# A hybrid decoder step on eight cores: sample tile amid the prompt groups, paced loads, FFN buffers laid over mixer buffers, two planner settings

## The chip, the cores and the metric

The kernel runs on the 8 cores of one Trainium2 chip. Each core works on one sequence of the prompt and on its share of the sample tokens. The time is the device time of the slowest core. The fast runs of one kernel agree within 0.3% (the kernel before) to 0.8% (e_pw) here; some runs fall in a slower state, in which the cores of one die, sometimes of both, show a lower granted clock (the clock that TensorE was allowed). The engine with the most work is TensorE (the matmul engine); the others are VectorE (DVE), ScalarE (ACT), GpSimd (POOL) and SyncE (SP), which issues loads and stores, as GpSimd does.

## The reference, cut to what matters

```python
def _layer(h, pe, state, ...):                  # one layer, DEPTH = 1
    a = rmsnorm(h, norm_mix)
    z = a @ w_in                                # 1024 -> 3080: [u | v_g | q | k | v_m | o | i | f]
    u = gelu(u); vg = layernorm(gelu(vg), ...)  # vg of the last chunk is an output: o_Vp, o_Vs
    y_gm = _gmlp_mix(u, vg, ...)                # causal 128x128 mixing, 4 heads
    hm, state = _mlstm(q, k, vm, ig, lf, state, ml_len)   # matrix memory C (4 heads, 128x128)
    h = h + concat([y_gm, sigmoid(o) * rmsnorm(hm)]) @ w_out
    h = h + square(relu(rmsnorm(h, norm_ffn) @ w_up)) @ w_down      # 1024 -> 4096 -> 1024
    gate = sigmoid(rmsnorm(h, norm_ple) @ w_ple_gate)
    h = h + gate * (pe @ w_ple_proj)
    return h, state, vg
# then a final rmsnorm. Prompt: 8 x 2048 tokens, zero state. Sample: 128 x 8 tokens, carried state.
```

A core has 16 prompt tiles of 128 tokens and one sample tile of 16 sequences with 8 tokens each. The sample tile needs its carried memory `state_C` (`sC` below), which is 16 x 4 matrices of 128x128 in fp32.

## The kernel before

The 17 tiles go in two halves: 8 prompt tiles and the sample tile, then 8 prompt tiles. In a half, the mixer stages (input norm N, projections P, gates G, mixing M) run in groups of two tiles, then the FFN runs in four quarters of its width, and stage C (gate, final norm, output `y`) follows the last quarter.

The kernel is a program that plans a program. Every operation is put on a list; a greedy planner with a cost model then fixes one static order for each engine, and semaphores are placed after it. The planner has a model of loads and a number of accumulation banks (those that TensorE writes its results to) that each class of operations may hold; any edit of the kernel gives another order everywhere.

```python
            if o.dma:                                   # in Plan.schedule: one queue for all loads
                free[e] = s + o.cost
                d0 = max(free[e] + 1.0, dma_free)
                dma_free = d0 + o.nbytes / 170e3        # 170 GB/s on the bytes of the destination
                o.fin = dma_free + 1.2
...
        order = P.schedule(dict(P=3, M=4, N=1, U=3, D=2, C=2, X=2))    # banks by class; N: norm transposes
...
        SO = Arena(W_OFF + 32 * KB, W_OFF + 48 * KB)    # state buffers ON two weight slots (k, m)
        CSB = [SO.bf(16 * 130, ...) for _ in range(2)]
        R = Arena(0, W_OFF)                             # FFN and stage C, laid over A
        ...
        A3 = [R.bf(DM) for _ in range(2)]               # norm buffers of stage C
        A2T = R.bf(8 * 9 * 128, k8(8))                  # FFN input, nine tiles in one piece
        ABF = [R.bf(DM) for _ in range(2)]              # norm buffers of the FFN
        A = Arena(0, W_OFF)                             # mixer
        ...
        VO = A.f32(512)                                 # output vg, its own buffer
        ABA = [A.bf(DM) for _ in range(2)]              # norm buffers of the mixer
...
            groups = [sg[0:2], sg[2:4], sg[4:6], sg[6:8]] + ([sg[8:9]] if len(sg) > 8 else [])
            for gi_, grp in enumerate(groups):
                ...                                     # load_x, stage_N, stage_P, stage_G, stage_M
            load_q(0)                                   # FFN weights of quarter 0
```

Of the kernel before, what the change touches and what calls it, by code (L numbers as in the profile page):

```python
# [19 lines left out]
def _dsize(dt):  # L20
    return mybir.dt.size(dt)
# [102 lines left out]
class Emit:  # L124
# [112 lines left out]
    def op(self, eng, calls, reads, writes):  # L237
        deps, rr, wr = self._deps_for(reads, writes, eng)
        self._emit_waits(eng, self._waits(eng, deps))
# [14 lines left out]
        self._record(rr, wr, tok, eng)  # L254

    def dma(self, eng, kw, out, in_):
        deps, rr, wr = self._deps_for([in_], [out], "dma")
        i = self.dma_i[eng]
# [15 lines left out]
        self._record(rr, wr, tok, "dma")  # L274

# [33 lines left out]
class Op:  # L309
    __slots__ = ("eng", "dma", "calls", "reads", "writes", "cost", "nbytes", "idx", "rank", "preds", "succs", "npred",  # L310
                 "pts", "tset", "fin", "tready")
# [9 lines left out]
class Plan:  # L321
# [3 lines left out]
    def __init__(self):  # L325
        self.ops = []
        self.bufs = {}
        self.boost = 0

    def add(self, eng, calls, reads, writes, cost, dma=False, nbytes=0, tset=None):  # L330
# [4 lines left out]
        o.rank = o.idx - self.boost  # L335
# [6 lines left out]
    def _link(self, o):  # L342
        P = o.preds
        psr = {}
# [41 lines left out]
    def schedule(self, caps):  # L386
# [28 lines left out]
        while len(order) < n:  # L415
# [48 lines left out]
            if o.dma:  # L464
                free[e] = s + o.cost
                d0 = max(free[e] + 1.0, dma_free)
                dma_free = d0 + o.nbytes / 170e3
# [27 lines left out]
DM = 1024  # L495
# [9 lines left out]
def build():  # L505
# [29 lines left out]
    with ExitStack() as st:  # L535
# [78 lines left out]
        def dma(out, in_, eng="sp", **kw):  # L614
            nb = _nelem(out) * list(out.ap)[0][1] * _dsize(out.dtype)
            return P.add(eng, (out, in_, kw), [in_], [out], 0.9 if eng == "pool" else 0.06, dma=True, nbytes=nb)
# [83 lines left out]

        W_OFF = ARENA - 65536
# [12 lines left out]
        SO = Arena(W_OFF + 32 * KB, W_OFF + 48 * KB)  # L714
        CSB = [SO.bf(16 * 130, ("p (j e) -> p j e", dict(j=16)))[:, :, 0:129] for _ in range(2)]
        QTD = SO.bf(16 * 128, ("p (j t) -> p j t", dict(j=16)))

        R = Arena(0, W_OFF)
        WG = R.bf(8 * DM, k8(8))
        WP = R.bf(2 * DM, k8(2))  # L720
        NF = R.f32(DM)
        A3 = [R.bf(DM) for _ in range(2)]
        A3T = [R.bf(8 * 128, k8(8)) for _ in range(2)]
        PBF = [R.bf(PLE) for _ in range(2)]
        PTT = [R.bf(2 * 128, k8(2)) for _ in range(2)]
        TC = [R.f32(DM) for _ in range(2)]
        Z2 = R.off
        A2T = R.bf(8 * 9 * 128, k8(8))
        ABF = [R.bf(DM) for _ in range(2)]
        GT = [R.bf(8 * 384, k8(8)) for _ in range(2)]  # L730
        RL = [R.f32(384) for _ in range(2)]
        SU = Arena(Z2 - 18 * KB + 2 * KB, Z2)
        CSF = [SU.f32(8 * 129, ("p (j e) -> p j e", dict(j=8))) for _ in range(3)]
        KMK = SU.bf(8 * 128, ("p (j d) -> p j d", dict(j=8)))
        NOUT = SU.f32(64, ("p (h j) -> p h j", dict(h=4)))

        A = Arena(0, W_OFF)
# [9 lines left out]
        VO = A.f32(512)  # L747
        BROW = A.f32(512)
        SBS = A.f32(512, h4)
        KTOK = [A.bf(512, h4) for _ in range(3)]  # L750
        VAUG = [A.bf(4 * 130, h4)[:, :, 0:129] for _ in range(4)]
        UT = [A.bf(4 * 256, h4) for _ in range(2)]
        SGT = [A.bf(4 * 256, h4) for _ in range(2)]
        QT = [A.bf(4 * 256, h4) for _ in range(2)]
        KT = [A.bf(4 * 256, h4) for _ in range(2)]
        XH = [A.bf(512) for _ in range(3)]
        VN = [A.f32(512) for _ in range(2)]
        AT = [A.bf(8 * 256, ("p (k n) -> p k n", dict(k=8))) for _ in range(2)]
        ABA = [A.bf(DM) for _ in range(2)]


        dma(H[:, 0, :], xp[0:128, :])
        dma(GN[:], gains)
        dma(IDB[:], cident, eng="pool")

        def load_win(names):
            v = w_in.rearrange("(k p) n -> p k n", p=128)
# [519 lines left out]
```

## Time and profile before

| | before |
|---|---|
| median of 4 runs (range) | 1049.41 us (1047.43 to 1106.67, the last one slow) |
| profiled span, slowest core | 1052.3 us |
| TensorE busy | 895.6 us (85%) |
| TensorE idle | 157 us |
| first `y_p` store issued | 510.6 us |
| first FFN matmul (384 columns) | 279.69 us |

The prediction below shows the stretches in which TensorE stands idle. Two more lines of the page complete them. The first pair is the chain of waits that sets the end, by engine and by what it waited for; the third line, of the list of loads (the four that the mixer waits for), gives a load's kilobytes and its median time from issue to landing.

```profile
PE 75%; DMA 11%; DVE 6%; issue 4%; POOL 2%; ACT 1%; another core or an unknown queue 0%; DVEq 0%; POOLq 0%; ACTq 0%
PE pb L251 75%; DMA WGT<-wgate 5%; DMA AR<-sC 4%; DVE AR L251 3%; DMA AR<-psm 2%; ACT AR L251 1%; POOL SMALL L251 1%; DVE ROWX L251 1%; POOL AR L251 1%; DVE H L251 1%; DVE SMALL L251 0%; POOL AR L273 0%; DVE CST L251 0%; DVE ROWN L251 0%
...
AR<-sC POOLq DMA_DIRECT2D x4, 512.0 KB, 26.1
```

A quarter of this chain is not matmul work, and 11% of the span is waiting for loads: the gate weights at the start, the state `sC`, and the sample's `psm` (its per-layer embedding) at the handover between the halves.

One mark is used in all that follows: the issue of the first `y_p`. It divides a run into a **first part** (start, first mixer, first FFN) and a **second part** (handover, second mixer, second FFN, end). In the kernel before, these parts are 510.6 and 1052.3 - 510.6 = 541.7 us. The *handover* is the stretch in which the first half's stage C meets the second half's norms and projections; the *second transition* is that from the second mixer to the second FFN.

### The profile page before, as it was taken

The page shows a single profiled execution, that of the slowest core. Times are in us where ns is not written, and L with a number is a line of the kernel's source. Part 1 is how long each engine was busy: PE and PEld are TensorE (multiplying, and loading weights), DVE is VectorE, ACT ScalarE, POOL GpSimd, SP SyncE. Part 2 cuts the span into 40 slices and gives each one's busy share as a digit, 9 for nine tenths or more (in the row PEclk, how much of TensorE's full clock was granted, in tenths as well). Part 3 has the DMA queues.
Part 4 walks back from the last instruction along what each step waited for, and adds up shares of the span by engine and source line. Part 5 has one row for each costly group of instructions (what it writes and reads, how often), then busy time and mean ns, then how long its engine had stood idle before and what let it go on. Part 6 is the DMA issues. An engine that isn't in the chain of part 4 may idle for free.

```text
span 1052.3 us, 17095 instructions; the slowest of 8 cores (1034.6 to 1052.3 us)
## 1 busy us (share of the span) xinstructions
PE 895.6 (85%) x5875; PEld 535.8 (51%) x5875; DVE 587.3 (56%) x1092; ACT 383.5 (36%) x706; POOL 265.7 (25%) x383
## 2 busy tenths in 40 slices
PE   0588899622799999999998797799699999999994
PEld 0365577411554555555554476466355555555552
DVE  2184987912655744444666334899664444444665
ACT  2564544410521112213456444345451211213543
POOL 4141543712401201001133221556520101000221
PEclk9999999865899999999999699699799999999998
DMA  9993000989995917246239500005997725400121
GB/s 170 215 154 54 1 2 2 115 81 126 187 193 89 185 43 122 40 57 106 87 87 202 135 21 1 1 1 91 125 126 124 105 55 83 78 1 3 46 69 60
DMA packets 80769, 90.62 MB, mean 86 GB/s; under 512 B 13736, under 2 KB 62124, under 8 KB 80684
## 3 DMA queue, kind: packets, MB, share of 16 engines
q0 software_dynamic: 54304, 59.22, 40.3%
q1 hardware_dynamic: 26380, 30.32, 10.1%
q8 instruction: 48, 0.79, 0.3%
q14 instruction: 37, 0.30, 0.1%
HBM read 134.81 MB, written 13.93 MB: 141 GB/s over the span
## 4 chain that ended last, share of the span: by engine, by line
PE 75%; DMA 11%; DVE 6%; issue 4%; POOL 2%; ACT 1%; another core or an unknown queue 0%; DVEq 0%; POOLq 0%; ACTq 0%
PE pb L251 75%; DMA WGT<-wgate 5%; DMA AR<-sC 4%; DVE AR L251 3%; DMA AR<-psm 2%; ACT AR L251 1%; POOL SMALL L251 1%; DVE ROWX L251 1%; POOL AR L251 1%; DVE H L251 1%; DVE SMALL L251 0%; POOL AR L273 0%; DVE CST L251 0%; DVE ROWN L251 0%
## 5 line engine op out<-in xcount | busy, mean ns | idle before, releaser
L251 PE MATMUL pb<-AR 128*128 128x512 bf16 (+4 forms) x4924 | 837.9, 330 | 72.5 <-DMA AR<-sC 32.4
L251 PEld LDWEIGHTS pb<-AR 128*128 128x128 bf16 x4924 | 469.2, 99 | 408.4 <-issue 99.9
L251 ACT ACTIVATE AR<-pb 128x384 f32<-128x384 f32 (+5 forms) x349 | 176.4, 512 | 458.6 <-PE pb L251 377.3
L251 DVE TENSOR_TENSOR H<-H,pb 128x512 f32<-128x512 f32 x170 | 116.5, 685 | 143.1 <-PE pb L251 142.9
L251 DVE TENSOR_TENSOR AR<-AR 128x384 bf16<-128x384 f32 (+2 forms) x209 | 123.0, 591 | 113.9 <-ACT AR L251 113.3
L251 ACT ACTIVATE AR<-H 128x1024 bf16<-128x1024 f32 x68 | 71.5, 1052 | 65.8 <-DVE H L251 26.1
L251 PE MATMUL pb<-IDB,AR 128*128 128x128 bf16 x578 | 51.7, 234 | 51.2 <-ACT AR L251 34.8
L251 DVE TENSOR_TENSOR AR<-pb,GN 128x1024 bf16<-128x1024 bf16 x51 | 61.7, 1221 | 60.2 <-PE pb L251 59.8
L251 POOL TENSOR_SCALAR SMALL<-SMALL 128x1 f32<-128x1 f32 x85 | 22.8, 268 | 286.2 <-ACT AR L251 246.6
L251 POOL TENSOR_TENSOR SMALL<-SMALL,NEGH 128x1 f32<-128x1 f32 (+1 forms) x102 | 69.9, 686 | 37.2 <-DVE SMALL L251 18.3
L251 PEld LDWEIGHTS pb<-IDB,AR 128*128 128x128 bf16 x578 | 41.8, 105 | 65.8 <-issue 56.9
L251 ACT ACTIVATE AR<-H,SMALL 128x1024 bf16<-128x1024 f32 x51 | 58.1, 1145 | 32.3 <-POOL SMALL L251 32.0
L273 POOL DMA_DIRECT2D AR<-w_up x16 | 14.6, 914 | 148.6 <-PE pb L251 141.3
L251 DVE TENSOR_TENSOR AR<-pb,AR 128x258 f32<-128x258 f32 (+3 forms) x86 | 43.4, 521 | 2.9 <-PE pb L251 1.7
L251 ACT ACTIVATE AR<-pb,GSM 128x129 f32<-128x129 f32 x68 | 20.4, 369 | 51.0 <-PE pb L251 50.9
L251 DVE SCALAR_TENSOR_TENSOR AR<-AR,pb 128x512 f32<-128x512 f32 x34 | 23.2, 684 | 22.3 <-PE pb L251 11.5
L251 ACT ACT_TABLE_LOAD x24 | 30.8, 1283 | 11.5 <-PE pb L251 5.0
L251 ACT ACTIVATE AR<-AR 128x512 f32<-128x512 f32 x34 | 21.4, 629 | 31.9 <-DVE AR L251 31.4
L251 DVE SCALAR_TENSOR_TENSOR AR<-H,SMALL,AR 128x1024 f32<-128x1024 f32 x17 | 22.7, 1338 | 10.2 <-POOL SMALL L251 10.1
L251 POOL TENSOR_TENSOR AR<-AR,GROW 128x512 bf16<-128x512 f32 (+1 forms) x19 | 24.7, 1306 | 12.8 <-DVE AR L251 10.5
L273 POOL DMA_DIRECT2D AR<-w_in x12 | 10.8, 905 | 62.4 <-PE pb L251 62.3
L251 POOL TENSOR_TENSOR AR<-MSK,GSM 128x512 f32<-128x512 f32 x17 | 18.3, 1079 | 32.8 <-DVE GSM L251 32.8
(100 smaller groups left out, 437.0 us busy)
## 6 DMA issues: line engine op xcount, KB each, us to landing
AR<-w_up POOLq DMA_DIRECT2D x16, 1024.0 KB, 13.9
AR<-w_down POOLq DMA_DIRECT2D x16, 1024.0 KB, 15.6
AR<-w_in POOLq DMA_DIRECT2D x12, 1024.0 KB, 21.6
H<-xp SPq DMA_DIRECT2D x16, 512.0 KB, 10.5
y_p<-AR SPq DMA_DIRECT2D x16, 512.0 KB, 3.0
AR<-w_out POOLq DMA_DIRECT2D x2, 2048.0 KB, 50.8
AR<-sC SPq DMA_DIRECT2D x8, 512.0 KB, 16.9
o_Cs<-AR SPq DMA_DIRECT2D x8, 512.0 KB, 5.0
```

What stands on the lines that cost most here:

```text
L251: ins = getattr(e, name)(**kw)
L273: lambda e, out=out, in_=in_, sem=sem, kw=kw: e.dma_start(out=out, in_=in_, **kw).then_inc(sem, 16))
```

## The change

Its intent: load only what is wanted next and hold the rest until a mark is reached; move the sample tile before the last prompt group, with state buffers of its own, loaded ahead; lay the FFN's input over mixer buffers that come free early, so that the FFN can start while the mixer ends. It also changes the planner's model of loads and its number of norm banks. The diff, cut to its core:

```diff
-                dma_free = d0 + o.nbytes / 170e3
+                dma_free = d0 + o.nbytes / 290e3       # and nb = 4 bytes per element, the fp32 source
...
-        CSB = [SO.bf(16 * 130, ...) for _ in range(2)]      # on weight slots
-        A3, ABF, ABA: a pair of norm buffers for each of the three stages; VO, BROW: own buffers
+        AB = [LOW.bf(DM) for _ in range(2)]                 # ONE pair for all three
+        CSB = [A.bf(8 * 130, ...) for _ in range(2)]        # own, half a head each
+        B_ = Arena(P0, FO[1]);  A2T = [B_.bf(8 * 384, g3) for _ in range(2)]   # over AT and VN
+        B_ = Arena(FO[1], FO[0]);  GT = [...]; RL = [...]   # over u, o, q, k of the other parity
+        B_ = Arena(FO[0], XO);  A2T.append(B_.bf(8 * 384, g3)); ...
...
-                    dma(o_Vs if t["ty"] == 1 else o_Vp, VO)
+                    dma(o_Vs if t["ty"] == 1 else o_Vp, vn) # vn = VN, under the FFN's input
...
+                elif gi_ > 1:
+                    for t in grp:
+                        load_x(t, marks[gi_ - 2])           # wait for an earlier group's gelu
...
+                    load_win("v", after=nops[:1])           # nops: the scaling of a norm
+                    consts_a(nops[1:]);  wgate, load_win("o", after=nops[1:])
+                    load_win("qkm", after=nops);  w_out
+                if si == 0 and gi_ == 2:
+                    sample_prep(marks[1])                   # state tiles, their norms and constants
...
-            groups = [sg[0:2], sg[2:4], sg[4:6], sg[6:8]] + ([sg[8:9]] if len(sg) > 8 else [])
+            groups = [sg[0:2], sg[2:4], sg[4:6]] + ([sg[8:9]] if len(sg) > 8 else []) + [sg[6:8]]
...
-        order = P.schedule(dict(P=3, M=4, N=1, U=3, D=2, C=2, X=2))
+        order = P.order = P.schedule(dict(P=3, M=4, N=2, U=3, D=2, C=2, X=2))
```

A load with an `after` is called *paced* below. The planner counts the load as not startable before its mark, and the issuing engine waits for the mark's semaphore.

## The prediction

> **What bounds the kernel now.** I read the page first, in its slices, then stretches of the span one by one, then the chain of waits, then the timeline inside the three worst stretches.
>
> ```profile
> PE 895.6 (85%) x5875; PEld 535.8 (51%) x5875; DVE 587.3 (56%) x1092; ACT 383.5 (36%) x706; POOL 265.7 (25%) x383
> ...
> PE   0588899622799999999998797799699999999994
> ...
> PEclk9999999865899999999999699699799999999998
> DMA  9993000989995917246239500005997725400121
> ```
>
> One digit is 26.3 us. TensorE is at 9 nearly everywhere except five places: the first two slices, slices 8 to 10, some digits around slices 21 to 28, and the last. So no engine binds overall; the kernel is TensorE work (895.6 us) plus 157 us in which TensorE stands still. The DMA row says what is odd: it is at 9 during the first 75 us, then 0 for 100 us, and then at 9 just where TensorE has its 2s. Loads come in lumps, too early or too late.
>
> The stretches put numbers on this (columns: stretch, its length, busy time of TensorE, weight loads, VectorE, ScalarE and GpSimd with counts, granted clock, DMA share, GB/s):
>
> ```profile
> 0.00:105.00 105.00, 61.89 (x480) 44.76 (x480) 43.47 (x87) 48.87 (x77) 34.34 (x69) 1.00 0.86 148
> 105.00:184.00 79.00, 74.14 (x639) 53.13 (x640) 67.89 (x160) 39.75 (x77) 35.78 (x40) 1.00 0.01 2
> 184.00:280.00 96.00, 42.38 (x354) 28.13 (x352) 48.25 (x116) 22.56 (x42) 39.56 (x42) 0.68 0.94 121
> 280.00:545.00 265.00, 263.79 (x1500) 141.24 (x1498) 139.75 (x234) 77.41 (x146) 34.86 (x52) 1.00 0.56 103
> 545.00:606.00 61.00, 49.08 (x276) 26.20 (x275) 32.10 (x39) 32.60 (x53) 18.57 (x38) 0.86 0.76 163
> 606.00:673.00 67.00, 53.95 (x441) 39.67 (x440) 35.92 (x75) 30.18 (x55) 21.57 (x31) 0.88 0.02 9
> 673.00:735.00 62.00, 60.71 (x468) 41.40 (x466) 56.24 (x136) 29.58 (x61) 33.20 (x37) 0.96 0.22 32
> 735.00:775.00 40.00, 26.71 (x180) 14.74 (x181) 27.12 (x49) 15.76 (x31) 19.50 (x27) 0.79 1.04 126
> 775.00:1016.00 241.00, 240.63 (x1428) 135.94 (x1425) 117.18 (x183) 73.09 (x145) 22.44 (x40) 1.00 0.39 67
> 1016.00:1053.00 37.00, 22.33 (x122) 10.57 (x122) 19.42 (x23) 13.74 (x26) 5.87 (x13) 0.91 0.17 62
> ```
>
> Length minus TensorE busy is the idle time, row by row: 43.1, 4.9, 53.6, 1.2, 11.9, 13.1, 1.3, 13.3, 0.4, 14.7 us. The FFN halves are dense (263.79 of 265): nothing to gain there. The clock column shows a second loss: where TensorE idled, it then worked at a lowered clock.
>
> What it waits for in the worst stretches, from the chain of waits (start, us, what) and the timeline:
>
> ```profile
> 4.03 47.94 DMA WGT<-wgate
> ...
> 209.17 43.73 DMA AR<-sC
> ...
> 566.93 23.34 DMA AR<-psm
> ```
>
> ```profile
> 249.11 1.89 PE L251 MATMUL pb<-AR 128*128 128x129 bf16 x16 [30.41 <-DMA AR<-sC]
> ...
> 265.33 1.09 PE L251 MATMUL pb<-AR 128*128 128x129 bf16 x16 [0.34 <-DVE AR L251]
> ```
>
> At the start, the gate weights and the second pair of input tiles take their share of a full queue (203 GB/s moved in the first 40 us); ScalarE waited 14.37 us for `H<-xp`, and projections begin only at 40.45 us. At 249.11 TensorE ends 30.41 us of idling for the carried state `sC` of the sample tile, issued at 201.07 us behind four FFN weight loads of 1024 KB each and landed 47.9 us after issue. The last two lines are the same 16 matmuls, 1.89 us just after a stall, 1.09 us later.
>
> **What the Trainium skill says.** "TensorE: Matmul & The Clock Gate", section "What's actually happening": the array's unworked state is half clock, and it falls back after an idle window of about 3.4 us. The trace agrees: 0.68 granted in 184 to 280 us, and the pair above. So each long stall costs twice. "DMA: Bandwidth & Descriptors", section "Issuing engines are not separate DMA queues": transfers of all issuers run on the same 16 DMA engines and interleave. The trace agrees: `sC` takes 47.9 us for 512 KB when weights are in flight, while the fastest load of this tensor took 5.2 us. Same page, "Why small descriptors are slow (HBM only)": small descriptors carry fixed overhead. `sC` is read in rows of 128 floats; the slices in which it shares the queue show 81 and 126 GB/s against 187 to 202 for weights alone, which fits. "Perfetto Trace Analysis", section "Optimization Strategy": regimes with different limits may gain by interleaving. That is the idea of this change: the sample tile (state loads) goes among prompt tiles (TensorE and VectorE work, DMA share 0.01).
>
> **Part 1, loads paced at the start.** Removed from the first queue: `v`, the gate weights, constants, tiles 2 to 7, the sample tile, `sC`'s normaliser. Now only x tiles 0 and 1, gains, identity and the `u` slab come at once: 0.5 + 0.5 + 1.05 MB plus small ones = 2.1 MB, at 203 GB/s 10.4 us, landing near 13 us. Tile 0's chain stays: its x landed by 6.2 us, transposes at 11.70, copy at 12.82. GpSimd's dozen memsets move to VectorE, a little earlier rsqrt. Tile 1's transposes ran at 15.16 us before, but its copy waited on VectorE until 21.98 behind an operation that waited for a constant; that is gone. So `u` projections can begin near 17.5 us instead of 40.45. They then meet loads: `v` with tiles 2 and 3 (2.1 MB from about 12 us) lands near 24, `o` with gate weights and a broadcast row (1.6 MB) near 32, then q, k, m at about 5.2 us each. A slab serves 32 matmuls of 256 columns per group, 32 x 0.109 = 3.5 us (an estimate: in 16 matmuls of 1.91 us and 32 of 3.65 the second 16 add 1.74), and two groups are ready by 30 us, so 7 us of work per slab exceeds 5.2 us of load (1.05 MB at 203 GB/s): after 30 us loads stay ahead of TensorE. Loss in the stretch to 105 us: 16 idle + 2.5 + 1.5 waiting + 3 slow clock + 6 of mixer friction as now = 29. Now: 43.1 + 4 of slow clock = 47. Gain 18.
>
> **Part 2, sample tile amid the first half.** Its PE work (projection, 64 state matmuls, mixing) stays. Its loads run when the queue is empty (share 0.01 from 105 to 184). The state buffers no longer lie on the k and m weight slots, so they are loaded ahead. Losses now in 105 to 280: 4.9 + 53.6 idle, and some 10 us of slow clock (42.38 us at 0.68 would be 29 at full clock if all were slow; the matmul pairs suggest 10) = 68. After: mixer friction 8, state reloads 7, transition to the FFN 5 = 20. Gain 48.
>
> **Part 3, FFN buffers over early-free buffers.** Before, the normalised FFN input lay over u, o, q, k tiles of both parities, so no FFN tile could start until the last mixer group ended. Now two of three tile groups lie over AT and VN, which the last projection frees; FFN matmuls can fill the last mixer group. This is the 735 to 775 stretch (13.3 + 4 clock = 17, to 8: gain 9) and the 5 us in part 2. On the way back, the next half's projection input lies over the first two FFN groups instead of their relu squares, so projections can fill the C stage at 545 to 606, where `psm` is awaited 23.34 us: 11.9 + 5 = 17, to 7: gain 10. In 606 to 673 (13.1 + 5 = 18) the serial gate chain remains, with more left to put beside it: gain 6. Gate and final-norm weights load later, in a half-empty queue: nothing either way. The end, 14.7 us, stays.
>
> Sum: 18 + 48 + 9 + 10 + 6 = 91; 1050.35 - 91 = 959 us.
>
> **Rivals.** (a) The `sC` wait moves with the tile. Four heads in two half buffers mean six reloads behind matmuls; the planner now reckons 290 GB/s on f32 bytes, about 4 us for 0.5 MB with its fixed terms, but 5.2 us was this tensor's best landing. If TensorE's fixed order meets each 3 to 5 us too early, 20 to 30 us come back: 980. For it: the in-order engine; against: an idle queue. (b) VectorE binds the mixer: 67.89 of 79 us (86%) in 105 to 184, and the sample tile adds to it. Over the first-half mixer, about 160 us of VectorE in some 215 is 74%, so locally only: 970. (c) The start is bound by bytes: 8 MB of projection weights have to come whatever the order; then part 1 brings 8 instead of 18: 969. (d) The handover stretches fill entirely: 54 us of losses from 545 to 775 fall by 40, not 25: 944.
>
> **Range and chances.** TensorE work at full clock is about 895.6 - 28 = 868; with 16 us of start and 15 of end, 900 is a floor. (a) and (c) together give near 990, (d) with a good sample tile near 935. Range 935 to 985. Even part 2 at half its size beats 2% (21 us), so faster 0.97.
>
> **What would show it.** First 256-column projections near 18 us; no TensorE wait for `sC` over 5 us; clock near 1.0 between 180 and 270 us; the first 384-column matmul near 214 us (279.69 - 18 - 48) instead of 279.69, starting before the last mixer group's output projection; no 23 us `psm` piece in the chain; TensorE busy near 870. I am wrong if the wait reappears on `sC`, on FFN weights arriving after the mixer, or on VectorE above 90% in the mixer.

## More of the kernel before

The norm used everywhere takes a bank of class N for its transposes:

```python
        def norm_T(g, so, hsrc, abf, dst, goff, junk=None):
            ...
            act(abf if junk is None else junk, hsrc, AF.Square, accum=ss)
            rstd(rs, tmp, ss, 1.0 / DM, EPS)
            act(abf, hsrc, AF.Copy, scale=rs)
            p = psb("N")                                # 8 transposes into one bank, one copy out
```

## The result, and the profile after

The changed kernel takes 1019.94 us (median of 4 runs, 1017.47 to 1022.47), against 1049.41 before: a ratio of 0.9725, with a 95% interval of 0.9691 to 0.976. A ratio here is the mean time of one kernel's runs over that of the other's of the same rounds, so it isn't quite the ratio of the medians. Executions in which one die ran at a lower clock are left out of the means. It is faster, by about 30 us instead of the 91 predicted, and outside the range.

From the page after, in the same order as before: TensorE's line, its slices, the granted clock and the loads' share, then the chain. One slice is 25.5 us.

```profile
PE 895.8 (88%) x5807; PEld 539.0 (53%) x5875; DVE 581.2 (57%) x1118; ACT 391.8 (38%) x711; POOL 264.4 (26%) x370
...
PE   2578898937999999999997678998899999999994
...
PEclk9798899967999999999999889999999999999997
DMA  9993010996677768065249400003999909000111
...
PE 75%; DMA 9%; DVE 6%; issue 5%; ACT 3%; POOL 2%; DVEq 0%; SPq 0%; POOLq 0%; ACTq 0%
PE pb L252 75%; DVE AR L252 3%; DMA AR<-sC 3%; DMA AR<-w_in 3%; DMA AR<-pp 2%; ACT AR L252 2%; POOL SMALL L252 1%; DMA H<-xp 1%; DVE H L252 1%; DVE SMALL L252 1%; DVE ROWX L252 1%; ACT L252 1%; POOL AR L252 0%; DVE ROWR L252 0%; POOL CST L252 0%
```

The zero at the start is gone, but the third slice went from 8 to 7 and the next two stayed at 8. The double 2 of the sample tile is now one 3. The handover still has its dip, now as 7, 6, 7 where 8, 7, 9, 7, 7 stood; the 6 of the second transition is gone. In the chain the gate weights have gone, and `w_in`, `sC` and `pp` stand in their place. TensorE's busy time did not fall to 870: it is 895.8 us, with 68 of 5875 matmul records missing, and the clock row still has its 6 and 7.

Stretches of 40 us of the changed kernel (columns as in the prediction: stretch, length, busy time of TensorE, weight loads, VectorE, ScalarE, GpSimd, then granted clock, DMA share, GB/s):

```profile
0.00:40.00 40.00, 16.91 (x111) 11.91 (x112) 11.99 (x32) 16.00 (x21) 15.90 (x29) 0.96 1.00 166
40.00:80.00 40.00, 28.93 (x207) 21.20 (x210) 18.31 (x49) 12.81 (x25) 10.09 (x12) 0.87 1.09 179
80.00:120.00 40.00, 30.76 (x216) 20.54 (x218) 26.82 (x61) 17.68 (x36) 17.77 (x22) 0.83 0.15 22
...
200.00:240.00 40.00, 18.51 (x132) 12.73 (x131) 18.29 (x37) 16.79 (x30) 14.38 (x21) 0.66 1.16 152
...
560.00:600.00 40.00, 24.52 (x134) 13.28 (x135) 17.66 (x20) 21.19 (x31) 13.37 (x22) 0.79 0.35 97
640.00:680.00 40.00, 37.97 (x306) 26.52 (x311) 36.43 (x88) 24.25 (x42) 17.34 (x22) 1.00 0.00 1
720.00:760.00 40.00, 36.42 (x270) 21.66 (x272) 33.40 (x58) 20.73 (x41) 19.82 (x27) 1.00 1.08 126
```

What it waits for there, from TensorE's timeline (start, duration, then in brackets the idle time just before and what ended it):

```profile
20.04 5.29 PE L252 MATMUL pb<-AR 128*128 128x256 bf16 x32 [1.58 <-DVE AR L252]
...
45.66 8.71 PE L252 MATMUL pb<-AR 128*128 128x256 bf16 x47 [6.67 <-DMA AR<-w_in]
...
218.80 1.03 PE L252 MATMUL pb<-AR 128*128 128x129 bf16 x8 [15.66 <-DMA AR<-sC]
...
590.88 1.01 PE L252 MATMUL pb<-IDB,AR 128*128 128x128 bf16 x8 [2.48 <-ACT AR L252]
```

The projections do begin at 20 us instead of 40, but the next weights come late, a wait of 15.66 us for the state `sC` is still there, and the last line is the first transposes of the second half's input norm, which stand at 590.88 us, just behind the issue of the sample's output at 588.8. Of the 32.0 us between the two profiled spans, 510.6 - 490.4 = 20.2 us come from the first part and 541.7 - 529.9 = 11.8 us from the second.

### The profile page after: what moved, and what is told of

Read it like the earlier page. It is cut to its first block, busy times and chain, and to the rows that moved or that the text cites. A ratio compares the mean times of both kernels' runs of the same rounds, so it can differ in the third digit from the quotient of the medians.

```text
span 1020.3 us, 17111 instructions; the slowest of 8 cores (1003.6 to 1020.3 us)
## 1 busy us (share of the span) xinstructions
PE 895.8 (88%) x5807; PEld 539.0 (53%) x5875; DVE 581.2 (57%) x1118; ACT 391.8 (38%) x711; POOL 264.4 (26%) x370
## 3 DMA queue, kind: packets, MB, share of 16 engines
q0 software_dynamic: 54224, 59.18, 40.9%
## 4 chain that ended last, share of the span: by engine, by line
PE 75%; DMA 9%; DVE 6%; issue 5%; ACT 3%; POOL 2%; DVEq 0%; SPq 0%; POOLq 0%; ACTq 0%
PE pb L252 75%; DVE AR L252 3%; DMA AR<-sC 3%; DMA AR<-w_in 3%; DMA AR<-pp 2%; ACT AR L252 2%; POOL SMALL L252 1%; DMA H<-xp 1%; DVE H L252 1%; DVE SMALL L252 1%; DVE ROWX L252 1%; ACT L252 1%; POOL AR L252 0%; DVE ROWR L252 0%; POOL CST L252 0%
## 5 line engine op out<-in xcount | busy, mean ns | idle before, releaser
L252 POOL TENSOR_SCALAR SMALL<-SMALL 128x1 f32<-128x1 f32 x85 | 26.3, 310 | 245.4 <-ACT AR L252 201.9
L252 DVE TENSOR_TENSOR AR<-pb,AR 128x512 f32<-128x512 f32 (+3 forms) x86 | 43.7, 523 | 9.4 <-ACT AR L252 8.4
L252 ACT ACT_TABLE_LOAD x29 | 37.2, 1283 | 16.1 <-PE pb L252 10.2
L252 POOL TENSOR_TENSOR AR<-AR,GROW 128x512 bf16<-128x512 f32 (+1 forms) x19 | 25.5, 1341 | 16.5 <-PE pb L252 8.5
L252 ACT ACTIVATE AR<-pb,GSM 128x129 f32<-128x129 f32 x68 | 20.7, 366 | 13.7 <-PE pb L252 13.5
L276 POOL DMA_DIRECT2D AR<-w_down x16 | 12.2, 765 | 51.4 <-PE pb L252 51.3
## 6 DMA issues: line engine op xcount, KB each, us to landing
AR<-w_in POOLq DMA_DIRECT2D x12, 1024.0 KB, 17.5
```

The source lines that it names most:

```text
L252: ins = getattr(e, name)(**kw)
L276: lambda e, out=out, in_=in_, sem=sem, kw=kw: e.dma_start(out=out, in_=in_, **kw).then_inc(sem, 16))
```

## The experiments

Eighteen kernels ran, all with correct results, each timed in three rounds beside the kernel before. They ran on several chips, on which the kernel before took from 1048 to 1057 us, so ratios are compared. "First part" and "second part" are read from the profiled run.

| run | design | ratio (95%) | first part | second part |
|---|---|---|---|---|
| (before) | | 1 | 510.6 | 541.7 |
| (after) | the change | 0.9725 (0.9691 to 0.976) | 490.4 | 529.9 |
| e_waitless | its order, run-time waits of pacing left out | 0.9717 (0.9692 to 0.9742) | 487.5 | 529.4 |
| e_null | the change, another order | 0.9778 (0.974 to 0.9815) | 489.8 | 537.3 |
| e_send | sample tile at the end, paced | 0.9743 (0.971 to 0.9775) | 489.9 | 533.8 |
| e_ab | stage C with its own norm buffers, paced | 0.9687 (0.9652 to 0.9722) | 486.6 | 530.6 |
| e_sc | FFN weights of the first quarter held for the state loads | 0.9835 (0.9792 to 0.9877) | 498.1 | 531.6 |
| e_x2 | third group's tiles loaded earlier | 0.9646 (0.9613 to 0.9679) | 476.9 | 534.7 |
| e_pw | only weights and constants paced | 0.968 (0.9637 to 0.9723) | 489.1 | 533.3 |
| e_px | only input tiles paced | 0.9621 (0.9588 to 0.9654) | 480.9 | 531.4 |
| e_ps | only state tiles paced | 0.9583 (0.9554 to 0.9612) | 478.5 | 531.6 |
| e_nopace | nothing paced | 0.9392 (0.9366 to 0.9418) | 455.8 | 528.3 |
| e_nopace_null | the same, another order | 0.9602 (0.9561 to 0.9644) | 470.5 | 536.0 |
| e_nopace_send | nothing paced, sample at the end | 0.96 (0.956 to 0.9641) | 471.6 | 535.3 |
| e_nopace_send_null | the same, another order | 0.9567 (0.9536 to 0.9597) | 475.5 | 531.0 |
| e_nopace_dmn1 | nothing paced, planner settings of before | 0.9694 (0.9662 to 0.9727) | 479.6 | 534.9 |
| e_nopace_ab | nothing paced, own norm buffers | 0.9414 (0.9392 to 0.9435) | 453.1 | 531.9 |
| e_best | the same, and o_Vp from another buffer | 0.9295 (0.9253 to 0.9336) | 455.7 | 513.4 |
| b_plan | the kernel before with both planner settings | 0.9765 (0.9737 to 0.9794) | 501.2 | 519.5 |
| b_n2 | the kernel before with two norm banks | 0.9728 (0.9695 to 0.9761) | 512.2 | 514.4 |

### First call: one part undone at a time

**e_nopace.** All pacing dropped; the planner makes a new order.

```diff
-        o.after, o.tok, o.tag = after, None, self.tag
+        o.after, o.tok, o.tag = (), None, self.tag
```

> Edit: all pacing waits on loads are dropped; everything else stays. Theory (the start is bound by bytes): projections start near 20 us with pacing but then wait for slabs, so the pacing is worth little: 1010 to 1028, and the sum of TensorE idle time up to 105 us stays within 8 us of the 40 us that the paced kernel has. Rival (as predicted): pacing is worth 18 us, and the time becomes 1035 or more.

Measured: 987.35 us, ratio 0.9392, below both of my expectations. So pacing, which was to bring 18 us at the start, costs 33 us in this pair of kernels (1019.94 - 987.35), nearly all of it in the first part (490.4 against 455.8). The tiles' loads share the queue with the weights again, and projections start at 21.42 us all the same. (Part of the 33 us is the luck of the order.)

**e_send.** The sample tile goes back to the end of the half.

```diff
-            groups = [sg[0:2], sg[2:4], sg[4:6]] + ([sg[8:9]] if len(sg) > 8 else []) + [sg[6:8]]
+            groups = [sg[0:2], sg[2:4], sg[4:6], sg[6:8]] + ([sg[8:9]] if len(sg) > 8 else [])
```

> Edit: the sample tile goes back to the end of the first half; own state buffers, pacing and FFN layout stay. Theory (the order matters): most of the gain of the first half comes from having prompt tiles to work on during the state reloads; with the tile at the end four reloads of about 8 us are exposed again: 1038 to 1050. Rival (buffers matter): what made the old wait long was that the state buffers lay on weight slots and the FFN weights went first; with own buffers the place does not matter: 1012 to 1026.

Measured: 1024.39 us, ratio 0.9743, which overlaps the change's own interval. With the loads paced, the move that was to bring most of 48 us brings nothing that these runs can show.

**e_sc.** The weights of the FFN's first quarter wait until the last state load has landed.

```diff
-            load_q(0)
+            load_q(0, list(csl) if si == 0 else ())    # csl: the last load of sC; w_up, w_down wait for it
```

> Edit: the four loads of the first FFN quarter are not issued before the last state load of the sample tile has landed. Theory (queue sharing): the state reload issued at 190.57 us took 28 us only because FFN weights of 1024 KB each were in flight; now every state reload lands within 9 us, the 15.7 us wait of TensorE for sC goes, and the time falls by about 10 us to 1010. Rival (exchange): TensorE then waits for w_up instead, because those loads begin some 20 us later; the time stays within 1015 to 1026, with a wait on w_up of 10 us or more.

Measured: 1033.6 us, ratio 0.9835, slower than the change. The state waits did shrink, to 0.55, 3.38 and 2.64 us on the timeline, but the first `y_p` moved from 490.4 to 498.1, and both expectations missed. The wait of 10 us for `w_up` that my rival named isn't there. The edit did less than I meant: two loads of `w_up` left at 206.16 us, ahead of the last four state loads (219.51 to 227.15 us). By the code they can only be the second quarter's, which it doesn't hold. The loss stands later: from 320 to 360 us TensorE is busy for 33.45 us, against 39.75 in the changed kernel. There VectorE, in e_sc, waits 9.94 us for another load of `sC` (for the update of the state), which was issued after a store of 15.88 us. How much of all this is the new order I can't say; holding the weights back was no gain here.

**e_ab.** Stage C gets its own pair of norm buffers again.

```diff
+        A3 = [R.bf(DM) for _ in range(2)]
-            norm_T(n, 36, hsl, AB[par], A3T[par], G_PLE)
+            norm_T(n, 36, hsl, A3[par], A3T[par], G_PLE)
-            act(AB[par], hsl, AF.Square, accum=ss)
+            act(A3[par], hsl, AF.Square, accum=ss)
```

> Edit: the last stage (gate and final norm) gets two norm buffers of its own again, instead of the pair AB that it shares with the input norms of the second half. Theory (false sharing): the second half's first norms wait for the last tile's final square, which reads AB, so its projections start at 593 us, after the first half's last output; with own buffers the first 128x256 matmuls of the second half begin before 575 us, the idle time of TensorE between 540 and 600 us falls from 20 us to under 8, and the time falls by 12 to 20 us, to about 1004. Rival (late loads): the second half's weights and the per-layer inputs set the start; then the time stays within 1016 to 1023.

Measured: 1019.7 us, ratio 0.9687: no change in the median. The rival's number came, but not its cause (late loads): the trace shows an improvement that was then lost. The handover was better (the sample's output is issued at 574.8 us, not 588.8, and TensorE is full from 580 on), but at the second transition VectorE, writing the FFN's input, waited 14.64 us for the store of `o_Vp`. The change had removed the buffer `VO` and stores this output from `VN`, over which the FFN's input lies.

### Second call: run time or order, and the noise of the order

**e_waitless.** The order is exactly that of the changed kernel; only the run-time waits of the paced loads are left out.

```diff
-                o.tok = E.dma(o.eng, kw, out, in_, [q.tok for q in o.after])
+                o.tok = E.dma(o.eng, kw, out, in_, [])
```

> Edit: the planned order of every engine is exactly that of the changed kernel; only the extra semaphore waits of the paced loads are left out when the program is emitted, so each paced load is issued as soon as its queue's engine reaches it. The run without pacing (987 us) also got a newly planned order, so this one separates the two. Theory (the pacing costs by holding loads back at run time: o, q, k, m weights issued at 18.8 to 24.5 us instead of earlier, the state tiles behind them): at least half of the 33 us comes back, 1000 us or less, and the first stretch to 120 us loses at least 15 us less. Rival (the planner, which counts the paced loads as late, places the norms and projections of the third group late, and that fixed order is what costs): the time stays within 1 per cent of the changed kernel's 1020 us, since the engines still come to each instruction in the same order.

Measured: 1019.18 us, ratio 0.9717: the rival held. Loads went out earlier, TensorE's 20 to 40 us became worse and its 60 to 80 us better, and the time stayed. The reason shows in the transposes of the third group's norm. The three fences are the changed kernel, this run, and the run without pacing.

```profile
96.32 1.01 PE L252 MATMUL pb<-IDB,AR 128*128 128x128 bf16 x8 [3.23 <-DVE AR L252]
```

```profile
96.40 1.01 PE L252 MATMUL pb<-IDB,AR 128*128 128x128 bf16 x8 [3.24 <-DVE AR L252]
```

```profile
36.32 1.01 PE L252 MATMUL pb<-IDB,AR 128*128 128x128 bf16 x8 [9.09 <-ACT AR L252]
```

With or without the waits the third group is normalised at 96 us, because the planner had put it there when it counted that group's input as late. An engine takes its instructions in the order of its list: the Trainium skill says so in "PSUM — Partial Sum Buffer", section "Engine vs sequencer instructions" (the queues of ScalarE, VectorE and GpSimd are strict FIFO, and matmuls start in program order), and this pair of runs agrees, 96.32 against 96.40 us. A load that lands early helps nobody whose place in the list is late.

**e_null.** Nothing of the design is changed; a latency constant of the planner goes from 0.22 to 0.23 us, which gives another order.

```diff
-CROSS, SAME = 0.22, 0.06
+CROSS, SAME = 0.23, 0.06
```

> Edit: nothing of the design; one constant of the planner's cost model (its latency between engines, 0.22 to 0.23 us) is changed, which gives another static order of the same instructions. It measures how far a time moves by the order alone. Expected on either theory: within 1 per cent (10 us) of the changed kernel's 1020 us. If it moves by more than 15 us, then the single edits that moved the time by 5 to 15 us (own norm buffers, the place of the sample tile, the held FFN weights) show nothing.

Measured: 1025.82 us, ratio 0.9778, so 0.5% from the change by the order alone (the intervals overlap). The differences of e_send and e_ab from the change are of that size, and as times they show nothing.

**e_nopace_ab.** The edits of e_nopace and e_ab together.

```diff
+ the two diffs above
```

> Edit: no pacing, and stage C has its own pair of norm buffers again, as before the change. Theory (the second half's projections wait for the last tile's use of the shared norm buffer, some 20 us of idle TensorE at the handover near 520 to 560 us of the unpaced kernel's 987 us): with the buffers apart the second half's projections start before the sample's output is issued, the handover loses 8 us or less, and the time is 965 to 978 us. Rival (the gap moves on, as in the run with own buffers and pacing, where the second handover lost what the first won because the vector output o_V is stored from a buffer that the FFN's input lies over): 982 to 990 us, with a loss of over 10 us between the second mixer and the FFN.

Measured: 987.61 us, ratio 0.9414: the rival held, as the gap moved on. The handover is repaired, but then one piece in the chain of waits stands out:

```profile
681.45 24.65 DMA o_Vp<-AR
```

It is a store of 256 KB that shares the DMA engines with the FFN's weights, and the FFN's input may not be written until it has left its buffer.

**e_nopace_send.** The edits of e_nopace and e_send together.

```diff
+ the two diffs above
```

> Edit: no pacing, and the sample tile goes back to the end of the first half; its state buffers stay its own. Theory (with the load queue not held up, moving the tile is worth little too, because the transition still waits for reloads of the state tiles behind the FFN weights, and the own buffers bring what the move was credited with): 985 to 1000 us, within 1.5 per cent of the unpaced kernel. Rival (the move is worth the 20 us or more of the prediction and the pacing hid it): 1005 us or more, with a TensorE idle stretch of over 15 us between the last prompt group and the FFN of the first half.

Measured: 1007.56 us, ratio 0.96. Against e_nopace that would make the sample's place worth 20 us once nothing is paced, with this line to go with it:

```profile
236.29 15.48 PE L252 MATMUL pb<-AR 128*128 128x384 bf16 x80 [18.69 <-DMA AR<-w_up]
```

In the chain this is one load of `w_up`, issued at 186.68 us and landed 49.48 us later, while the other FFN weights and, from 194.34 us on, state loads were in flight.

### Third call: a better version, and the planner's settings

**e_best.** As e_nopace_ab, and the prompt's vector output is formed in the sample's bias buffer, which is unused in the second half.

```diff
-                    brow = SQ.rearrange("p h t -> p (h t)")
+                    brow = (SQ if t["ty"] == 1 else SBS).rearrange("p h t -> p (h t)")
...
-                    tt("pool", vn, vn, brow, ALU.add)
-                    dma(o_Vs if t["ty"] == 1 else o_Vp, vn)
+                    vo = vn if t["ty"] == 1 else brow
+                    tt("pool", vo, vn, brow, ALU.add)
+                    dma(o_Vs if t["ty"] == 1 else o_Vp, vo)
```

> Edit: no pacing, own norm buffers for stage C, and the prompt's vector output o_Vp is formed in and stored from the sample's bias buffer (unused in the second half) instead of the tile buffer that the FFN's input lies over. In the run without the last edit the handover at 520 to 560 us was repaired (5 us of idle TensorE in place of 15), but TensorE then lost 25 us at 660 to 720 us, where the chain shows a 24.65 us store of o_Vp. Theory (the FFN's input waits for that store because of the shared buffer, and nothing else holds the second transition): the stretch 640 to 720 loses 8 us or less, and the time is 960 to 972 us. Rival (the second transition is held by the FFN weights or the output sums in any case, and the store only came last): 980 us or more, with the loss still over 15 us there.

Measured: 973.73 us, ratio 0.9295, faster than both kernels and just above the range that I had expected. Three stretches of e_nopace_ab, then the same of e_best:

```profile
540.00:560.00 20.00, 18.02 (x140) 14.08 (x141) 9.51 (x17) 11.13 (x17) 4.24 (x6) 0.91 0.07 27
680.00:700.00 20.00, 15.54 (x97) 8.48 (x95) 4.32 (x8) 3.74 (x6) 4.03 (x7) 0.92 0.98 128
700.00:720.00 20.00, 10.69 (x59) 5.75 (x60) 10.76 (x15) 5.28 (x10) 0.75 (x2) 0.74 1.07 167
```

```profile
540.00:560.00 20.00, 17.05 (x147) 13.61 (x145) 9.55 (x17) 12.68 (x20) 5.27 (x9) 1.00 0.12 40
680.00:700.00 20.00, 20.00 (x116) 10.77 (x117) 11.73 (x20) 7.83 (x13) 6.16 (x9) 0.87 0.96 90
700.00:720.00 20.00, 20.00 (x109) 10.53 (x108) 8.80 (x15) 3.49 (x8) 0.00 (x0) 1.00 1.06 178
```

The handover was already good in both (without own buffers, e_nopace had 11.90 of 20 us there, at a clock of 0.84). The second transition, which lost 14 us of TensorE in these two stretches, is full in them; over all of 640 to 720 us the loss fell from 25.4 to 10.5 us, where I had expected 8 or less. Own norm buffers alone had not moved the time (e_nopace against e_nopace_ab): the wait for the store had hidden their gain. The other buffer for the store was not run alone.

**b_plan.** The kernel before with the change's planner settings and nothing else.

```diff
-                dma_free = d0 + o.nbytes / 170e3
+                dma_free = d0 + o.nbytes / 290e3
-            nb = _nelem(out) * list(out.ap)[0][1] * _dsize(out.dtype)
+            nb = 4 * _nelem(out) * list(out.ap)[0][1]
-        order = P.schedule(dict(P=3, M=4, N=1, U=3, D=2, C=2, X=2))
+        order = P.schedule(dict(P=3, M=4, N=2, U=3, D=2, C=2, X=2))
```

> Edit: the kernel before with nothing but the change's planner settings, that is 290 GB/s on fp32 source bytes in its model of the DMA queue and two norm banks in flight for one; buffers, load order and the place of the sample tile stay as before. It asks how much of the 41 us that the unpaced kernel with the sample at the end has over the kernel before comes from the static order and not from buffers. Theory (buffers and the reordered loads): within 1 per cent of 1048 us, 1040 to 1060. Rival (the new order): 1030 us or less.

Measured: 1023.85 us, ratio 0.9765: the rival held. The two planner settings on the kernel before give nearly all that the whole change gives.

**e_nopace_dmn1.** The converse: the unpaced kernel with the settings of before.

```diff
-                dma_free = d0 + o.nbytes / 290e3         # and the bytes of the destination again
+                dma_free = d0 + o.nbytes / 170e3
-        order = P.order = P.schedule(dict(P=3, M=4, N=2, U=3, D=2, C=2, X=2))
+        order = P.order = P.schedule(dict(P=3, M=4, N=1, U=3, D=2, C=2, X=2))
```

> Edit: the unpaced kernel (987 us) with the planner settings of the kernel before (170 GB/s on destination bytes, one norm bank in flight). It is the converse of the run of the kernel before with the new settings. Theory (settings matter little beside buffers and places): 980 to 1000 us. Rival (the settings bring much of the gain): 1005 us or more.

Measured: 1017.4 us, ratio 0.9694: the rival held here too. By parts, it loses in the first (479.6) and hardly in the second (534.9, within the 528 to 537 of all kernels with the change's layout). Against the second order of the unpaced kernel (0.9602) the loss in time is less than 1%.

**e_x2.** All is paced, but the third group's two input tiles wait for the mark of the weights q, k, m in place of the later one.

```diff
-                elif gi_ > 1:
+                elif gi_ > 2:
...
+                    for t in groups[2]:
+                        load_x(t, nops)
```

> Edit: paced as in the change, but the two input tiles of the third group are loaded under the same mark as the weights q, k, m, in place of waiting for the first group's gelu, some 20 us later in the plan. Theory (the planner put the third group's norms at 90 us because it counted their load as late, so the engines had only the second group's mixing to do from 80 to 120 us, and this is the larger part of what pacing costs): the stretch 80 to 120 loses at least 6 us less than the 9 us of the changed kernel and at a clock of 0.9 or more, and the time is 1000 to 1010 us. Rival (the loss is in the late weights o, q, k, m themselves, or elsewhere in the order): within 1 per cent of 1020 us.

Measured: 1011.76 us, ratio 0.9646: just above the theory's range and just inside the rival's. The first part falls by 13.5 us to 476.9. But the stretch 80 to 120 lost 6.5 us (33.53 busy of 40) in place of 9.2, so not where I had expected it, and part of the reason remains order.

### Fourth call: which paced loads, which setting

**e_pw, e_px, e_ps.** One family of paced loads each. The diffs drop the marks of the other two.

```diff
+ e_pw: load_x(t, ()) for later groups; sample_prep(())
+ e_px: after=() for weights, constants and the second group's tiles; sample_prep(())
+ e_ps: after=() for weights, constants and all input tiles
```

> Edit: of the three families of paced loads only the first is paced (first-period weights v, o, q, k, m, the gate and output weights, the second group's tiles, the constants); the later input tiles and the sample's state tiles are not. The whole pacing cost 33 us (1020 against 987), and none of it came from waiting at run time. Theory (the weights' pace makes the planner order the first and second group's projections behind late weights, and this is what is left after the third group's late tiles, which brought 8 us): 1000 to 1012 us. Rival (the start's pace is harmless and the cost lies with the tiles and the state loads): 985 to 995 us.

> Edit: only the input tiles of the third and later groups of the first half wait for their mark; all other loads are unpaced. Theory (late tiles put the third group's norms late in the plan): 992 to 1000 us, with a thin stretch at 80 to 120 us. Rival (they cost nothing when the queue is filled early by the rest): 985 to 990 us.

> Edit: only the sample's state tiles, their norm column and its mixing constants wait for their mark (the second group's gelu). Theory (with the start unpaced the mark comes at 50 to 60 us, so the state tiles land long before the sample needs them at 175 us and the pace costs nothing): 985 to 993 us. Rival (they then land between the loads of the first period, whose order they change): 995 us or more.

Measured: 1021.97, 1015.15 and 1011.69 us, ratios 0.968, 0.9621 and 0.9583 (on a chip with the kernel before at 1056.6). The first two lie outside both of their expectations; for e_ps the rival held. Against e_nopace each family alone brings back most of the loss, so the costs do not add up. Against the second order of the unpaced kernel (0.9602, 0.9561 to 0.9644), though, e_px and e_ps can't be told from no pacing by their ratios; in its first part e_pw (489.1 us) lies with the paced kernels, while e_px (480.9) and e_ps (478.5) lie just above the unpaced ones (up to 475.5). Each has its own mark in its trace, here from e_pw, e_px and e_ps in turn:

```profile
50.13 5.12 PE L252 MATMUL pb<-AR 128*128 128x512 bf16 x16 [22.16 <-DMA AR<-w_in]
```

```profile
98.19 1.01 PE L252 MATMUL pb<-IDB,AR 128*128 128x128 bf16 x8 [2.70 <-DVE AR L252]
```

```profile
206.22 1.02 PE L252 MATMUL pb<-AR 128*128 128x129 bf16 x8 [18.01 <-DMA AR<-sC]
```

Paced weights leave TensorE waiting 22.16 us for one of them. Paced tiles put the third group's norm back to 98 us. Paced state tiles bring a wait of 18.01 us for `sC`, where the unpaced kernel waited 10.5 us for it in all.

**b_n2.** The kernel before with two norm banks alone.

```diff
-        order = P.schedule(dict(P=3, M=4, N=1, U=3, D=2, C=2, X=2))
+        order = P.schedule(dict(P=3, M=4, N=2, U=3, D=2, C=2, X=2))
```

> Edit: the kernel before with one of the change's two planner settings alone, two norm banks in flight for one; its model of the load queue stays at 170 GB/s. Both settings together brought 25 us (1024 against 1049). Theory (two norm banks let the transposes of the next tile run while the first is copied out, at both handovers, where norms of nine tiles come one behind the other): 1028 to 1036 us, so more than half. Rival (the load model does it, by placing the issue of loads and norms otherwise): 1042 us or more.

Measured: 1028.35 us on the slower chip, ratio 0.9728: the theory's range held, and the norm banks bring the whole of what both settings brought. Two stretches after the handover, before the edit and after it:

```profile
560.00:600.00 40.00, 29.45 (x154) 14.75 (x153) 18.98 (x21) 22.29 (x37) 11.90 (x26) 0.79 0.84 182
640.00:680.00 40.00, 28.09 (x183) 16.09 (x181) 31.23 (x70) 17.87 (x35) 16.24 (x18) 0.74 0.00 1
```

```profile
560.00:600.00 40.00, 33.55 (x227) 19.39 (x225) 23.24 (x27) 30.06 (x48) 14.51 (x28) 0.96 0.90 199
640.00:680.00 40.00, 39.02 (x300) 26.49 (x299) 34.35 (x81) 16.93 (x33) 15.76 (x18) 1.00 0.00 1
```

TensorE gains 4 us in the first and 11 in the second, and the clock goes to 0.96 and 1.00; the first part is unchanged (512.2 against 510.6). From 560 to 600 us, where stage C's norms and the second half's input norms meet, TensorE does nine sets of eight norm transposes in place of five. So with one bank the input norms queue with stage C's, and by 640 us less mixing is prepared; a trace does not show the bank itself, so this link is read from the edit.

### Fifth call: was the good order luck?

**e_nopace_null, e_nopace_send_null.** The planner's constant of e_null on e_nopace and on e_nopace_send.

```diff
-CROSS, SAME = 0.22, 0.06
+CROSS, SAME = 0.23, 0.06
```

> Edit: the unpaced kernel (ratio 0.939, 987 us against 1049) with the planner's latency constant at 0.23 for 0.22 us, so another static order of the same instructions. Theory (pacing costs some 30 us): a ratio to the kernel before of 0.95 or less, as the order alone moved the paced kernel by 0.6 per cent. Rival (the 987 us came from one lucky order, and paced kernels, at ratios of 0.958 to 0.978, are of the same family): a ratio of 0.955 or more.

> Edit: the unpaced kernel with the sample tile at the end (ratio 0.960), with the same changed constant. Theory (the sample tile's place is worth some 20 us when nothing is paced): a ratio 0.012 or more above that of the other run of this call. Rival (the 20 us were the order's luck): within 0.008 of it, or below.

Measured: ratios 0.9602 and 0.9567. Of e_nopace_null's five runs the fast two took 1008.02 and 1009.5 us. Both rivals held. The unpaced design has ratios of 0.9392 and 0.9602 in two orders, so 2.1 points from the order alone, and with the sample tile at the end it has 0.96 and 0.9567. The 20 us of the tile's place were within that.

What survives is this. In the first part of the profiled runs, the fully paced designs with the change's FFN weights (after, e_waitless, e_null, e_send, e_ab) lie at 486.6 to 490.4 us and the unpaced ones with the change's settings at 453.1 to 475.5. These two groups don't overlap, whatever the order or the tile's place. So pacing costs 19.3 us in one like pair (489.8 to 470.5, both under the constant 0.23) and 34.6 us in the other (490.4 to 455.8, both under 0.22). The tile's place, unpaced, shows 455.8 against 471.6 and 470.5 against 475.5, so 5 to 16 us from two pairs: a hint, not a finding.

## Why the prediction was wrong

The prediction was 66 us in the first part and 25 in the second. Measured were 20.2 and 11.8. Direction and class were right; the size was three times too large, and steps failed in each of its three parts.

**Part 1, the pacing, "Gain 18".** The first number in it was right: projections from 20.04 us, predicted 17.5. What failed is "after 30 us loads stay ahead of TensorE": after a wait for weights of 4.01 us, up to 29.33, one of 6.67 us ends at 45.66, and a piece of 26.73 us of `w_in` stands in the chain. In the stretch to 105 us TensorE idles 40.9 us, against 43.1 before and some 26 in the sum, at a clock of 0.90 instead of 1.00. The queue moved 166 and 179 GB/s in the first two stretches of 40 us, where the sum took 203. And the step took a paced load for a load that is only later at run time. It is also late in the plan, and the plan fixes the order of all engines (e_waitless). Without pacing projections start at 21.42 us, so the early start came from the change's other edits (the new list of loads, most likely) and not from the marks. In place of +18 stands a cost of some 20 to 35 us in the first part.

**Part 2, the sample tile, "state reloads 7", "transition 5", "friction 8".** Rival (a) was the true one, in another form than I gave it: not TensorE meeting each reload too early in an empty queue, but the reloads queued behind FFN weights again (`sC` behind `w_up` and `w_down`, a load of 27.98 us in the chain, a TensorE wait of 15.66 us). In 200 to 240 us TensorE has 18.51 us at a clock of 0.66, against the near-1.0 I named as the sign. The first FFN matmul came at 234.69 us instead of 279.69: 45 of the 66 us predicted up to there. But this does not carry through: the first `y_p` is only 20.2 us earlier. An earlier first FFN matmul is also an effect of the new buffers, which let FFN tiles start while mixer work is still outstanding; a milestone of one instruction is not a measure of work done. "Gain 48" can't be set beside a single measured number for the move; e_send gives nothing in the paced pair, and the unpaced pairs 5 to 16 us.

**Part 3, the buffers, "735 to 775: gain 9".** The sign here is right: 720 to 760 has 36.42 busy at clock 1.00, where before 735 to 775 had 26.71 of 40 at 0.79. Taken from 673 to 775 us in both, since the second transition came earlier, TensorE idles 6.6 us instead of 14.6. How much of it is the layout I can't say: counted from the first `y_p`, the stretch from 200 to 270 us idles 14.4 us before, 6.3 in the changed kernel and 12.7 in e_null, the same design in another order.

**Part 3, the way back, "gain 10" and "gain 6".** This is the step that failed. The sentence "projections can fill the C stage" looked only at where the FFN's big buffers lie and missed that the three pairs of norm buffers became one. The next half's norm must wait for the last use of that pair by stage C, and a gap of 40 - 24.52 = 15.5 us stands at 560 to 600; the `psm` piece of 23.34 us is gone from the chain, but a `pp` piece of 22.89 us stands there. That it is these buffers shows when the runs are laid over each other at their first `y_p`. From 60 to 100 us after it TensorE idles 9.0 us before and 17.1 in the changed kernel, so the change made this stretch worse. It idles 14.3 to 16.1 us in e_null, e_send, e_nopace and e_nopace_null, whatever the order, but 5.1, 5.0 and 4.2 in e_ab, e_nopace_ab and e_best, in which stage C has its own pair. The 606 to 673 stretch did fill (idle 5.3 us instead of 13.1), but the reason I gave ("the serial gate chain") was wrong: b_n2, in which only the norm bank differs from before, fills it as well (130 to 165 us after the first `y_p`: idle 1.0 us instead of 11.9).

**What the sum left out.** The diff's last line, N=1 to N=2, was given nothing. On the kernel before it alone makes the second part 541.7 - 514.4 = 27.3 us shorter, as much as I had given all of part 3 there. In the changed kernel the shared norm buffers then take most of it back. The second parts fall in two groups: 513.4 to 519.5 us (b_n2, b_plan, e_best), where stage C has norm buffers of its own and the store of `o_Vp` holds no buffer that the FFN needs, and 528.3 to 537.3 in all others that have the change's layout, e_ab and e_nopace_ab included, in which the store of `o_Vp` still blocks the FFN. So the change's own layout costs some 15 us of what its bank brings, and the two repairs together give it back. With one bank and the old model of loads, the unpaced kernel lies in the second group too (534.9), so there the two settings show no gain in the second part.

Of the rivals, (c) had the right place, but bytes alone do not set it: the queue is as full without pacing (a DMA share of 0.99 and 1.11 in the first two stretches of 40 us, against 1.00 and 1.09), and in 80 to 120 us TensorE is then busy for 38.27 us instead of 30.76. (b) did not bind, though its sign came: VectorE has 36.43 of 40 us (91%) at 640 to 680, but TensorE has 37.97 there. (d), 40 us less loss in the second part, came in no run; e_best's second part is 28.3 us shorter. And that `sC`'s short rows make it slow, which the prediction called fitting, no run tested. A slip of reading changes nothing: the DMA row before is at 0 for three slices, 79 us, not 100.

**What stays open.** The order alone moved one design by 2.1 points of its ratio, which is most of the change's 2.75. The kernel before was never run in a second order, so part of its 1049 us, and of what the second bank gains on it, may be its order; b_plan, two banks in another order, gains 22.2 us in the second part, where b_n2 gains 27.3. Two orders for a design are too few to give the pacing's cost, or the tile's place, to better than some 10 us. Also open is why three families of paced loads, each alone, cost nearly what they cost together; that e_nopace's own order was a lucky one is one way, but that is only argued. And e_best was timed in a single order, so its 973.73 us may hold luck in the first part (455.7 us, where e_nopace_null has 470.5).

## What to carry to other kernels

In a statically planned kernel a hint to one part is a change of the whole order: run the same design under a second order, by a change that means nothing, before you give a few per cent to a part of it. Count every pair of buffers that a diff merges as a wait between the stages that used them apart, and every output stored straight from a work buffer as one more; one such wait can hide another, so that a repair alone looks worthless. And price the one-character lines of a diff, since on the kernel before a second bank for a small, frequent step was worth nearly as much (2.7%) as the whole change.

## What the Trainium skill lacked or had wrong

- No page says that the order of a static plan can matter as much as its buffers. A latency constant of 0.23 instead of 0.22 us in the planner moved the unpaced kernel from a ratio of 0.9392 to 0.9602, and removing the run-time waits without changing the order moved nothing (0.9725 to 0.9717). It belongs to "Perfetto Trace Analysis", section "Optimization Strategy".
- The same section says that a repeating gap can mean too few buffers. It would gain from the case that the gap is seen far from the cause: the kernel before lost 12 us at 640 to 680 us, in mixing, and the cure was a second bank for norms (28.09 to 39.02 us of TensorE).
- "DMA: Bandwidth & Descriptors", section "Issuing engines are not separate DMA queues", says that DMAs interleave. It has no word on what this does to a store among loads, where the buffer it leaves is needed next: 256 KB of `o_Vp` took 24.65 us beside FFN weights (e_nopace_ab).
